# Moving the preparation of two transposed activations in a one-core transformer block: the memory's x^T earlier and later, the residual's x^T columns later

## The chip, the cores and the metric

The kernel runs on one core of a Trainium2 chip. The metric is the device time in microseconds of one execution; the median of three runs is given. The engines are named as in the profile: PE (matrix products), PEld (its weight loads), DVE (vector), ACT (scalar), POOL (general purpose) and SP (which issues most DMAs).

## The reference

One layer of a bidirectional encoder, all in float32, on 256 tokens of width 2048, with 256 memory tokens:

```python
x = x + concat([mla_attention(h), diff_attention(h)]) @ w_out    # h = rms_norm(x)
hx = rms_norm(x, g_xattn);  hm = rms_norm(mem, g_mem)
xq = hx @ w_xq              # (256, 512): queries, 4 heads of 128
xk = hm @ w_xk              # (256, 512): keys of the memory
xv = hm @ w_xv
x = x + softmax(xq xk^T / sqrt(128)) xv @ w_xo
x = x + (silu(hf @ w_gate) * (hf @ w_up)) @ w_down                # hf = rms_norm(x)
return rms_norm(x, g_final)
```

## The kernel before

**Products.** A float32 product is made of three faster ones: every operand is split into a high part, rounded by an ACT cast, and a low part, the rest, by a DVE subtraction, and PE adds high x high, high x low and low x high (lines 99 to 101). The function `split_into` makes the two parts: without a scale at lines 107 (ACT) and 108 (DVE), with a scale at 110 and 111. So each megabyte of weights, once landed in a buffer `wraw` (three of them), passes ACT and DVE as two casts into `wh` and two subtractions into `wl` (four buffers each) before PE can use it. A `wraw` buffer is free for the next DMA when its last subtraction is done.

**Order.** The program is written with tile pools, and the tile framework orders it when it is built: for each engine a planner simulates the time line, follows the order in the program as priority, and takes a later instruction where an earlier one isn't ready in its simulation. The order found is then fixed for each engine. Only the DMAs that SP issues for weights, the memory's x^T and the like are kept in the order of the program (`tc.keep_in_program_order`). Activations live in one pool, `act`, of 24 buffers of 4 KB a partition; a tile waits there until another one is released.

**The stretch that is changed.** The mix of the two attentions is multiplied by `w_out` in two halves of 1024 columns (`wide_add`, h = 0 and 1, called with `mix`). A half runs over eight pairs of 128-row blocks of the weights, in the order `OUT_ORDERS[h]`; for each one `before(n)` is called, then its megabyte is asked for. A pair of kind P is multiplied as it is; one of kind W uses sums of blocks of both operands (the tiles `tsum` and `forms`), which saves products on PE and costs additions on DVE. The half's result is added into the residual `x_res` (`join`, line 365, and `leave`, lines 354 to 362).

Then come the cross attention's keys, `project(mT, w_xk)`, in four pieces of 512 rows, each of them 24 matmuls of 512 columns; the mean squares of the memory's rows (`mss`, from tiles `mn` that POOL's DMAs bring at line 805) and the scaled and transposed keys; then the queries, `project(x1T, w_xq)`, also in four pieces; later the values, `project(mT, w_xv)`.

**What is prepared.** `mT` is the memory's x^T, already transposed in HBM, as four pieces of 512 rows. `mT.load(i)` issues the DMA of piece i on SP (line 408) into an `act` tile `xraw` and splits its four blocks with the gain: four ACT instructions `mT_h` (line 110) and four DVE instructions `mT_l` (line 111). Before, pieces 0, 1 and 2 are loaded ahead of the sixth, seventh and eighth pair of the first half, and piece 3 ahead of the first piece of the keys.

`x1T` is the residual's x^T, made on the chip. `x1_column(oc)` makes 512 rows of it out of 512 columns of `x_res`: for each of two token tiles four transposes on PE into `pt` (line 501), the product with the gain on DVE into `gT` (line 505), the split into `x1T_h` and `x1T_l`, and a square with a sum on ACT (line 203). Column oc is what piece oc of the queries reads. Before, columns 0, 1 and 2 are made ahead of the second, third and fourth piece of the keys and column 3 behind the keys; the reciprocal root of the residual's mean square (`rstdx`, in the profile `x1Tr`: a sum and an addition on DVE, a power on POOL) follows at once and is used when the queries are scaled.

Of the kernel before, what the change touches and what calls it, by code (L numbers as in the profile page):

```python
# [80 lines left out]
def encoder_block(ctx: ExitStack, tc: tile.TileContext, a, out):  # L81
# [15 lines left out]
    def mm(o, l, r, start, stop):  # L97

        nc.tensor.matmul(o, l.h, r.h, start=start, stop=False)  # L99
        nc.tensor.matmul(o, l.h, r.l, start=False, stop=False)  # L100
        nc.tensor.matmul(o, l.l, r.h, start=False, stop=stop)  # L101
# [13 lines left out]
    def act_tile(shape=(P, 4, S), name="act"):  # L115
        return Split(
            act.tile(list(shape), F32R, name=name + "_h", tag="act"),
            act.tile(list(shape), F32R, name=name + "_l", tag="act"),
        )

    def weights(src, fine=False, pool=None, before_k=None, cut=None, raw=None):

        nk, ncols = src.shape[1:]
        begun = raw is not None
        if not begun:
            raw = wp.tile([P, 2048], F32, name="wraw", tag="wraw", bufs=3)
        raw = raw[:, :nk * ncols].rearrange("p (k c) -> p k c", k=nk)  # L130
        step = 1 if fine else nk
        for k in range(0, nk, step):
            if before_k is not None:
                before_k(k)
            if begun and k == 0:
                continue
            tc.keep_in_program_order(nc.sync.dma_start(out=raw[:, k:k + step, :], in_=src[:, k:k + step, :]))
        ks = []
        step = max(1, 1024 // ncols // 2 * 2)
        for k in range(0, nk, step):  # L140
            n = min(step, nk - k)
            if pool:
                w = pool((P, n, ncols), "w")
            else:
                w = [wp.tile([P, 1024], F32R, name=x, tag=x, bufs=4)[:, :n * ncols].rearrange("p (k c) -> p k c", k=n)
                     for x in ("wh", "wl")]
                w = Split(*w)
            if fine:
                for j in range(n):
                    for c in ([slice(0, ncols)] if cut is None or k + j else [slice(0, cut), slice(cut, ncols)]):  # L150
                        split_into(w[:, j, c], raw[:, k + j, c])
            else:
                split_into(w, raw[:, k:k + n, :])
            ks += [w[:, j, :] for j in range(n)]
        return ks

    def project(actT, pieces, before=None, fine=0):

        accs = [acc_tile() for _ in range(NT)]
        ncols = pieces[0].shape[2]  # L160
        nk = sum(src.shape[1] for src in pieces)
        kt = 0
        for i, src in enumerate(pieces):
            if before is not None:
                before(i)
            for w in weights(src, i < fine):
                x = actT(kt)
                for tt in range(NT):
                    mm(accs[tt][:, :ncols], x[tt] if isinstance(x, tuple) else x[:, tt * P:(tt + 1) * P], w,
                       start=kt == 0, stop=kt == nk - 1)  # L170
                kt += 1
        return accs
# [4 lines left out]
    def nat(name):  # L177
        pool, bufs = nat_pool
        return pool.tile([P, 512], F32, name=name, tag="nat", bufs=bufs)
# [4 lines left out]
    def acc_tile(name="acc"):  # L184
        pool, tag = banks[0]
        return pool.tile([P, 512], F32, name=name, tag=tag)
# [5 lines left out]
    def rstd_of(ms, eps, name):  # L192

        cols = ms.shape[-1]
        r = small.tile([P, cols], F32, name=name, tag=name, bufs=2)
        nc.vector.tensor_scalar(out=r, in0=ms, scalar1=eps, scalar2=None, op0=ALU.add)
        nc.gpsimd.tensor_tensor(out=r, in0=r, in1=mhalf[:, :cols], op=ALU.pow)
        return r
# [147 lines left out]
    def wide_add(pairs, src, order, kinds, oc0, done=None, closed=(0, 1), before=None):  # L346


        def x(tt, oc):
            return x_res[tt][:, (oc0 + oc) * 512:(oc0 + oc + 1) * 512]  # L350

        def leave(Q):
            v, u = nat("v"), nat("u")
            nc.scalar.copy(out=u, in_=Q[1])
            nc.vector.tensor_tensor(out=v, in0=Q[6], in1=u, op=ALU.subtract)
            nc.vector.tensor_tensor(out=x(0, 0), in0=x(0, 0), in1=Q[1], op=ALU.add)
            nc.vector.tensor_tensor(out=u, in0=Q[5], in1=v, op=ALU.add)
            nc.vector.tensor_tensor(out=v, in0=v, in1=Q[7], op=ALU.subtract)
            nc.vector.tensor_tensor(out=x(1, 1), in0=x(1, 1), in1=Q[5], op=ALU.add)
            nc.vector.tensor_tensor(out=x(0, 1), in0=x(0, 1), in1=u, op=ALU.add)  # L360
            nc.vector.tensor_tensor(out=x(1, 0), in0=x(1, 0), in1=v, op=ALU.subtract)
            nc.vector.tensor_tensor(out=x(1, 1), in0=x(1, 1), in1=v, op=ALU.add)

        def join(tt, oc, acc):
            nc.vector.tensor_tensor(out=x(tt, oc), in0=x(tt, oc), in1=acc, op=ALU.add)
            if done is not None:
                done(tt, oc0 + oc)

        return wide_project(pairs, src, order, kinds, leave, join, closed, before)
# [236 lines left out]
    acc = project(lambda kt: cqT[:, kt, :], [a["w_uq_r"]])  # L606
# [163 lines left out]
    def column_T(t, oc, tt, gain, ssq, raw=None):  # L770

        xs = x_res[tt][:, oc * 512:(oc + 1) * 512]
        transposed(t, xs, tt, 4, gain[:, 4 * oc:4 * oc + 4], raw)
        meansq(xs, ssq[:, tt, oc:oc + 1], 512, D)

    def rstd_of_sums(ssq, name):
        s1 = small.tile([P, NT], F32, name=name + "s1", tag=name + "s1", bufs=1)
        nc.vector.reduce_sum(out=s1, in_=ssq, axis=AX.X)
        return rstd_of(s1, EPS, name + "r")

    mix = [Pair(t[:, k:k + 2, :]) for t in mixT for k in (0, 2)] + diff
    mT = Transposed(a["memT"], g_m, "mT")
    x1p = []
    x1ss = small.tile([P, NT, 4], F32, name="x1ss", tag="x1ss", bufs=1)
    for h in range(2):
        wide_add(mix, a["w_out"][h], OUT_ORDERS[h], OUT_KINDS[h], 2 * h,
                 before=lambda n: h == 0 and n >= 5 and mT.load(n - 5))

    def x1_column(oc):
        x1p.append(act_tile(name="x1T"))  # L790
        for tt in range(NT):
            column_T(x1p[oc], oc, tt, g_x, x1ss)
# [2 lines left out]
        return x1p[kt // 4][:, kt % 4, :]  # L795


    acc = project(mT, [a["w_xk"][i] for i in range(4)], before=lambda i: x1_column(i - 1) if i else mT.load(3))
    x1_column(3)
    rstdx = rstd_of_sums(x1ss, "x1T")  # L800
    mss = small.tile([P, NT, 4], F32, name="mss", tag="mss", bufs=1)
    for tt in range(NT):
        for c in range(2):
# [8 lines left out]
    for tt in range(NT):  # L812
        n = nat("xk")
# [1 line left out]
        transposed(xkT, n, tt, 4)  # L815


    acc = project(x1T, [a["w_xq"][i] for i in range(4)])
    xqT = act_tile(name="xqT")
    for tt in range(NT):  # L820
        n = nat("xq")
# [113 lines left out]
    for gi, (chunks, order) in enumerate(groups):  # L935
# [49 lines left out]
        for tt in range(NT):  # L985
            for h in range(2):
                acc = acc_tile("acc2")[:, :256]
# [98 lines left out]
```

## Time and profile before

| what | value |
|---|---|
| median of three runs | 1145.25 us (1145.14 to 1145.39) |
| the profiled execution | 1146.86 us, its span 1145.1 us |
| granted PE clock | 0.998 |
| instructions | 14370, 5390 of them matmuls |
| memory's x^T: first and last conversion on ACT | 268.5 and 319.4 us |
| residual's x^T: first and last split on DVE | 343.8 and 360.7 us |
| first matmul of the keys, of the queries | 332.25, 357.89 us |

The span is the time between the first and the last instruction; times within it are counted from its start. A row of the timeline gives the start, the duration, the engine, the line, the operation and the tiles, out<-in; a bracket at its end is the idle time of the engine before it, and what ended it. Rows that follow each other with the same tiles are merged, with their number.

### The profile page before, as it was taken

The page shows a single profiled execution, that of the slowest core. Times are in us where ns is not written, and L with a number is a line of the kernel's source. Part 1 is how long each engine was busy: PE and PEld are TensorE (multiplying, and loading weights), DVE is VectorE, ACT ScalarE, POOL GpSimd, SP SyncE. Part 2 cuts the span into 40 slices and gives each one's busy share as a digit, 9 for nine tenths or more (in the row PEclk, how much of TensorE's full clock was granted, in tenths as well). Part 3 has the DMA queues.
Part 4 walks back from the last instruction along what each step waited for, and adds up shares of the span by engine and source line. Part 5 has one row for each costly group of instructions (what it writes and reads, how often), then busy time and mean ns, then how long its engine had stood idle before and what let it go on. Part 6 is the DMA issues. An engine that isn't in the chain of part 4 may idle for free.

```text
span 1145.1 us, 14370 instructions
## 1 busy us (share of the span) xinstructions
PE 1134.2 (99%) x5390; PEld 947.5 (83%) x5390; DVE 980.3 (86%) x1339; ACT 648.3 (57%) x928; POOL 58.0 (5%) x75
## 2 busy tenths in 40 slices
PE   9999999999999999999999999999999999999997
PEld 7888888887878888888888888888888888888886
DVE  6688766878987767989899998998999898998975
ACT  6755455556556555656455565564554564654642
POOL 4920000000001000000000000000000000000000
PEclk9999999999999999999999999999999999999999
DMA  9655434545557444455555556555555555565553
GB/s 357 217 195 189 144 110 147 185 150 200 202 220 258 150 167 169 177 194 207 197 212 197 181 210 220 184 190 214 184 195 210 207 197 195 193 241 182 204 180 129
DMA packets 34197, 222.13 MB, mean 194 GB/s; under 512 B 4176, under 2 KB 4944, under 8 KB 9808
## 3 DMA queue, kind: packets, MB, share of 16 engines
q1 hardware_dynamic: 32688, 216.73, 53.0%
q0 software_dynamic: 864, 3.15, 0.8%
q10 hardware_dynamic: 576, 1.34, 0.3%
q8 instruction: 42, 0.69, 0.2%
q14 instruction: 27, 0.22, 0.1%
HBM read 219.11 MB, written 2.10 MB: 193 GB/s over the span
## 4 chain that ended last, share of the span: by engine, by line
PE 93%; DVE 4%; DMA 1%; issue 1%; ACT 0%; DVEq 0%; POOLq 0%; POOL 0%; ACTq 0%
PE acc L100 25%; PE acc L101 25%; PE acc L99 25%; PE q L100 3%; PE q L101 3%; PE q L99 3%; DVE wl L108 2%; PE pt L501 2%; DMA wraw<-in_w_dn 1%; PE ppt L649 1%; PE psc L100 1%; PE psc L101 1%; PE psc L99 1%; DVE tsum L301 0%; PE acckv L99 0%
## 5 line engine op out<-in xcount | busy, mean ns | idle before, releaser
L107 ACT CAST wh<-wraw 128x1024 fp32r<-128x1024 f32 (+2 forms) x400 | 389.3, 992 | 334.9 <-PE acc L101 288.7
L108 DVE TENSOR_TENSOR wl<-wraw,wh 128x1024 fp32r<-128x1024 f32 (+2 forms) x400 | 455.0, 1151 | 96.4 <-ACT wh L107 94.8
L107 ACT CAST wh<-tsum 128x1024 fp32r<-128x1024 f32 (+1 forms) x96 | 96.5, 1006 | 56.1 <-PE acc L101 26.0
L100 PE MATMUL acc<-wl,x2n_h 128*128 128x512 f32 x320 | 124.6, 390 | 0.0
L101 PE MATMUL acc<-wh,x2n_l 128*128 128x512 f32 x320 | 123.9, 389 | 0.0
L108 DVE TENSOR_TENSOR wl<-tsum,wh 128x1024 fp32r<-128x1024 f32 (+1 forms) x96 | 111.5, 1164 | 14.2 <-ACT wh L107 13.9
L99 PE MATMUL acc<-wh,x2n_h 128*128 128x512 f32 x320 | 109.7, 391 | 0.0
L100 PE MATMUL acc<-wl,x0T_h 128*128 128x512 f32 x224 | 88.8, 397 | 0.0
L101 PE MATMUL acc<-wh,x0T_l 128*128 128x512 f32 x224 | 88.5, 396 | 0.0
L99 PE MATMUL acc<-wh,x0T_h 128*128 128x512 f32 x224 | 87.5, 398 | 0.8 <-ACT x0T_h L110 0.8
L100 PE MATMUL acc<-wl,hT_h 128*128 128x512 f32 x188 | 73.4, 393 | 0.1
L100 PE MATMUL q<-wl,forms_h 128*128 128x512 f32 x187 | 72.8, 389 | 0.0
L101 PE MATMUL q<-wh,forms_l 128*128 128x512 f32 x187 | 72.6, 389 | 0.0
L101 PE MATMUL acc<-wh,hT_l 128*128 128x512 f32 x188 | 72.4, 390 | 0.0
L100 PEld LDWEIGHTS acc<-wl,x2n_h 128*128 128x128 f32 x320 | 60.1, 188 | 12.3
L101 PEld LDWEIGHTS acc<-wh,x2n_l 128*128 128x128 f32 x320 | 60.1, 188 | 12.4
L99 PEld LDWEIGHTS acc<-wh,x2n_h 128*128 128x128 f32 x320 | 59.9, 188 | 12.3
L99 PE MATMUL q<-wh,forms_h 128*128 128x512 f32 x187 | 65.6, 389 | 0.0
L100 PE MATMUL acc<-wl,forms_h 128*128 128x512 f32 x167 | 64.8, 389 | 0.0
L101 PE MATMUL acc<-wh,forms_l 128*128 128x512 f32 x167 | 64.8, 389 | 0.0
L99 PE MATMUL acc<-wh,hT_h 128*128 128x512 f32 x188 | 64.5, 391 | 0.0
L99 PE MATMUL acc<-wh,forms_h 128*128 128x512 f32 x167 | 62.9, 389 | 0.0
(405 smaller groups left out, 2245.3 us busy)
## 6 DMA issues: line engine op xcount, KB each, us to landing
wraw<-in_w_gate SPq DMA_DIRECT2D x44, 1024.0 KB, 4.8
wraw<-in_w_up SPq DMA_DIRECT2D x44, 1024.0 KB, 4.8
wraw<-in_w_dn SPq DMA_DIRECT2D x41, 1024.0 KB, 4.8
wraw<-in_w_in SPq DMA_DIRECT2D x24, 1024.0 KB, 4.8
wraw<-in_w_out SPq DMA_DIRECT2D x16, 1024.0 KB, 4.8
wraw<-in_w_in_lat SPq DMA_DIRECT2D x7, 832.0 KB, 7.3
wraw<-in_w_xk SPq DMA_DIRECT2D x4, 1024.0 KB, 5.1
wraw<-in_w_xq SPq DMA_DIRECT2D x4, 1024.0 KB, 4.9
```

Source lines behind the costliest of these rows:

```text
L99: nc.tensor.matmul(o, l.h, r.h, start=start, stop=False)
L100: nc.tensor.matmul(o, l.h, r.l, start=False, stop=False)
L101: nc.tensor.matmul(o, l.l, r.h, start=False, stop=stop)
L107: last_cast[0] = nc.scalar.copy(out=dst.h, in_=src).ins
L108: last_split[0] = nc.vector.tensor_tensor(out=dst.l, in0=src, in1=dst.h.bitcast(F32), op=ALU.subtract).ins
L501: nc.tensor.transpose(out=pt[:, j * P:(j + 1) * P], in_=src[:, j * P:(j + 1) * P], identity=ident)
L649: nc.tensor.transpose(out=pt[:, kt * S + tt * P:kt * S + (tt + 1) * P], in_=p[:, tt, kt * P:(kt + 1) * P], identity=ident)
```

## The change

Pieces 0 and 1 of the memory's x^T are loaded ahead of the fourth and the seventh pair of the first half (n = 3 and 6), pieces 2 and 3 ahead of the first and the second piece of the keys. Columns 0 and 1 of the residual's x^T are made ahead of the third and the fourth piece of the keys, columns 2 and 3 ahead of the second and third piece of the queries. The reciprocal root `rstdx` is asked for behind the queries.

```diff
     for h in range(2):
         wide_add(mix, a["w_out"][h], OUT_ORDERS[h], OUT_KINDS[h], 2 * h,
-                 before=lambda n: h == 0 and n >= 5 and mT.load(n - 5))
+                 before=lambda n: h == 0 and n in (3, 6) and mT.load(n // 3 - 1))
...
-    acc = project(mT, [a["w_xk"][i] for i in range(4)], before=lambda i: x1_column(i - 1) if i else mT.load(3))
-    x1_column(3)
-    rstdx = rstd_of_sums(x1ss, "x1T")
+    acc = project(mT, [a["w_xk"][i] for i in range(4)],
+                  before=lambda i: mT.load(i + 2) if i < 2 else x1_column(i - 2))
...
-    acc = project(x1T, [a["w_xq"][i] for i in range(4)])
+    acc = project(x1T, [a["w_xq"][i] for i in range(4)], before=lambda i: i in (1, 2) and x1_column(i + 1))
+    rstdx = rstd_of_sums(x1ss, "x1T")
```

## The prediction

> **What bounds the kernel now.** I read the page first (busy shares, then the chain that ended last), then the table of windows, to find the stretches in which the tensor engine is not full, then that engine's timeline and the chain of waits inside these stretches.
>
> ```profile
> span 1145.1 us, 14370 instructions
> ...
> PE 1134.2 (99%) x5390; PEld 947.5 (83%) x5390; DVE 980.3 (86%) x1339; ACT 648.3 (57%) x928; POOL 58.0 (5%) x75
> ...
> PE 93%; DVE 4%; DMA 1%; issue 1%; ACT 0%; DVEq 0%; POOLq 0%; POOL 0%; ACTq 0%
> ...
> 268.00:285.00 17.00, 16.25 (x70) 12.68 (x69) 16.72 (x28) 15.47 (x26) 0.00 (x0) 1.00 0.33 117
> 285.00:308.00 23.00, 23.00 (x103) 19.00 (x102) 22.26 (x31) 10.37 (x19) 0.00 (x0) 1.00 0.64 224
> 308.00:324.00 16.00, 15.47 (x67) 12.14 (x66) 14.43 (x22) 11.50 (x18) 0.00 (x0) 1.00 0.45 179
> 324.00:360.00 36.00, 36.00 (x175) 29.65 (x174) 33.72 (x46) 21.77 (x32) 3.03 (x5) 1.00 0.65 228
> ```
>
> The columns of a window are its length, then busy time of PE, PEld, DVE, ACT and POOL, the granted clock, and DMA. PE is busy nearly all the time, the chain is PE for 93%, and its clock is whole (1.00). So only what PE stands still for can be won. The change works on the stretch from the wide product with w_out over the memory's keys to the queries; of its windows shown here PE lacks busy time in two only, 268 to 285 and 308 to 324, at the end of either half of the wide product. DVE is nearly full in the first (16.72 of 17.00).
>
> A busy PE need not start matmuls at its rate, so the size of the holes comes from the starts. Timeline of PE, start and duration:
>
> ```profile
> 281.14 0.96 PE L99 MATMUL acc<-wh,diffT_h 128*128 128x512 f32 x3
> ...
> 284.50 0.50 PE L100 MATMUL acc<-wl,diffT_h 128*128 128x512 f32 x1 [0.25 <-DVE wl L108]
> 284.84 0.40 PE L101 MATMUL acc<-wh,diffT_l 128*128 128x512 f32 x1
> ...
> 320.24 0.39 PE L99 MATMUL q<-wh,forms_h 128*128 128x512 f32 x1
> ...
> 320.92 0.39 PE L99 MATMUL q<-pT_h,forms_h 128*128 128x512 f32 x1
> ...
> 323.51 0.50 PE L100 MATMUL acc<-wl,diffT_h 128*128 128x512 f32 x1 [0.39 <-DVE wl L108]
> 323.84 0.40 PE L101 MATMUL acc<-wh,diffT_l 128*128 128x512 f32 x1
> ...
> 332.25 0.61 PE L99 MATMUL acc<-wh,mT_h 128*128 128x512 f32 x2
> ...
> 333.16 0.40 PE L101 MATMUL acc<-wh,mT_l 128*128 128x512 f32 x1
> ```
>
> From 320.24 to 320.92 three matmuls start: 0.227 us each. Stall 1: ten start from 281.14 until 284.84, 3.70 us for 2.27, so 1.43 us are lost. Stall 2: eight from 320.92 until 323.84, 2.92 for 1.82, 1.10 lost. Stall 3, at the first keys: three from 332.25 until 333.16, 0.91 for 0.68, 0.23 lost. Together 2.76 us, 0.24% of the time: more than that the change can't win. 0.2% (2.3 us) is about what a measurement of this kernel can tell from no change.
>
> [...] By PE busy the two windows lack 0.75 + 0.53 = 1.28 us. By weight loads (19.00 of 23.00 in the full window, 12.68 of 17.00 and 12.14 of 16.00 in these) they lack 1.65 and 1.30, 2.95 us. [...]
>
> The chain of waits names what PE waited for:
>
> ```profile
> 269.05 0.97 ACT mT_h L110 x3
> 273.59 1.59 DVE mT_l L111 x4
> ...
> 279.32 0.86 DVE mT_l L111 x3
> ...
> 283.31 1.15 DVE wl L108
> ...
> 312.05 4.89 DMA wraw<-in_w_out
> ...
> 319.53 0.79 DVE mT_l L111 x2
> ...
> 322.32 1.15 DVE wl L108
> ```
>
> Three loads of the memory's x^T (mT, four ACT and four DVE instructions each) stand in front of the split weights (wl) that end stall 1, the fourth load in front of those that end stall 2.
>
> **The change part by part.** One load costs a third of this row, the window of stall 1 for the instructions on the tile xraw alone (length, then DVE and ACT):
>
> ```profile
> 268.00:285.00 17.00, 5.09 (x12) 5.11 (x12) 1.00 0.33 117
> ```
>
> So 1.70 us of DVE and 1.70 of ACT for a load (5.09/3 and 5.11/3).
>
> The queue, and the idle places into which loads move (SP, then DVE, then ACT; the bracket is the idle time before the row):
>
> ```profile
> 246.03 0.42 SPq L408 DMA_DIRECT2D xraw<-in_memT  x1
> 312.43 0.55 SPq L408 DMA_DIRECT2D xraw<-in_memT  x1
> 314.39 0.33 SPq L137 DMA_DIRECT2D wraw<-in_w_xk  x1
> 250.48 1.29 DVE L301 TENSOR_TENSOR tsum<-wraw 128x512 f32<-128x512 f32 x2 [3.66 <-DMA wraw<-in_w_out]
> 267.99 1.38 DVE L108 TENSOR_TENSOR wl<-tsum,wh 128x512 fp32r<-128x512 f32 x2 [1.57 <-ACT wh L107]
> 329.25 0.69 DVE L108 TENSOR_TENSOR wl<-tsum,wh 128x512 fp32r<-128x512 f32 x1 [1.57 <-ACT wh L107]
> 330.35 0.69 DVE L355 TENSOR_TENSOR v<-q,u 128x512 f32<-128x512 f32 x1 [0.41 <-ACT u L354]
> 268.55 1.70 ACT L110 ACTIVATE mT_h<-xraw,gains 128x256 fp32r<-128x256 f32 x4
> 318.23 1.71 ACT L110 ACTIVATE mT_h<-xraw,gains 128x256 fp32r<-128x256 f32 x4 [0.80 <-DMA xraw<-in_memT]
> ```
>
> Load 0, from the sixth pair to the fourth. Its DMA leaves SP ahead of the fourth pair's weights instead of at 246.03; the weights are pushed back by its 0.42 us of issue, or until a buffer of the pool is free, at the latest near 246. Its 1.70 us on DVE then fit before 250.48 (3.66 us idle) or, failing that, are caught up by 267.99 (1.57 idle). Taken: 0.
>
> Load 1 stays at the seventh pair: 0.
>
> Load 2, from the eighth pair to the front of the keys. It leaves stall 1's chain. With load 0 gone too, DVE and ACT have 2 x 1.70 = 3.40 us less to do ahead of the wl at 283.31; one load alone (1.70) would already cover 1.43. Gain of the two: between 0, if the planner's order keeps other work there, and 1.43; taken 1.43, since DVE and ACT work 16.72 and 15.47 of 17.00 us in that window and what leaves is larger than the hole. Late next is the wide product's second half, where DVE works 22.26 of 23.00 us; it enters it ahead by up to 3.40, PE by 1.43, so it doesn't become the bound.
>
> Stall 2: load 2 now has the place in the program and on SP that load 3 had (312.43, right behind the last pair's weights of 312.05), so the same four instructions stand in the same chain. Taken 0 of the 1.10; bounds, a gain of 1.10 if they find another place, a loss as priced under the second rival.
>
> Load 3, from the front of the keys to behind their first piece: its DMA follows the issue of 314.39, its work needs 1.70 us of DVE. Idle there are 1.57 and 0.41 us (329.25 and 330.35), together 1.98. Bounds: 0, if it falls into these, and 1.70, if it comes ahead of the wl that ends stall 3. Taken 0, near the idle time, as its matmuls come last of the four pieces.
>
> The x^T columns of the residual (x1_column): columns 0 and 1 come a piece later among the keys, 2 and 3 go into the queries. Each issues two groups of four transposes, two gains (gT), two casts, two splits and two squares; the number of all of them stays.
>
> ```profile
> 357.11 1.03 PE L501 MATMUL pt<-ident,xres 128*128 128x128 f32 x8
> 357.74 1.29 DVE L505 TENSOR_TENSOR gT<-pt,gains 128x512 f32<-128x512 f32 x2 [0.25 <-PE pt L501]
> 360.08 1.29 DVE L108 TENSOR_TENSOR x1T_l<-gT,x1T_h 128x512 fp32r<-128x512 f32 x2
> 367.46 1.23 DVE L108 TENSOR_TENSOR wl<-wraw,wh 128x1024 fp32r<-128x1024 f32 x1 [1.45 <-ACT wh L107]
> 352.27 0.69 POOL L197 TENSOR_TENSOR x1Tr<-x1Tr,mhalf 128x2 f32<-128x2 f32 x1 [95.70 <-DVE x1Tr L196]
> 352.90 2.40 POOL L805 DMA_DIRECT2D mn<-in_mem  x4
> 379.78 0.60 PE L501 MATMUL pt<-ident,xk 128*128 128x128 f32 x4
> ```
>
> A column takes 360.08 + 1.29 - 357.11 = 4.26 us from transposes to the last split. It is written one piece of the queries ahead of its use, 24 matmuls or 5.45 us, so it has 1.19 us to spare, more if its transposes slip into the keys. Its 2.58 us of DVE fit into idle stretches like that before 367.46 (1.45 us, one for each split). PE does the same transposes. Cost 0, cover: the queries' own matmuls.
>
> The reciprocal root x1Tr goes behind the queries, so the four loads of the memory's rows on POOL (352.90) stand behind it no more and may start earlier. Their squares and the scaled keys end before 379.78, where PE takes them up; earlier loads can only come into the way of other transfers. x1Tr is there some 26 us before 379.78 now and can be late by much of that. Cost 0.
>
> Sum: -1.43 + 0 + 0 + 0. The profiled execution took 1146.86 us (span 1145.1), 1.6 above the median of 1145.25; the difference applies to the median: 1145.25 - 1.43 = **1143.8 us**.
>
> **The rivals.** First, all three stalls go: with DVE 1.70 us lighter up to 324 and the keys' columns later, load 2 falls into idle time of ACT and stall 3 has no column beside it. For it: ACT is busy only 11.50 of 16.00 us there. Against: the load's place in program and queue is the old one. 1145.25 - 2.76 = 1142.5 us.
>
> Second, slower: the two loads side by side at the keys. Load 3's DMA stands behind a piece of weights; the last load's conversion already waited 0.80 us for its DMA (318.23). The 1 MB ahead of load 2 took 4.89 us, and load 2's wait ended 318.23 - 316.94 = 1.3 us behind it; so load 3 lands at about 314.39 + 4.89 + 1.3 = 320.6 (an estimate from these rows). If its conversions are queued right behind load 2's (ACT free at 319.94), ACT stands until 320.6 and then works 1.70: all casts behind are 2.4 us late, and DVE has 1.70 more. The worst is 2.4 + 1.7 = 4.1 us on stalls 2 and 3: 1145.25 - 1.43 + 4.1 = 1147.9 us. It decides once more than 1.43 of the 4.1 reach PE. For it: the order of each engine is planned before the run, and DVE works 33.72 of 36.00 us from 324 on. Against: the gaps for one more load are there. [...]
>
> Third, the change doesn't do what it says: the planner fills the room left in stall 1 with something else, or holds load 0 until a pool buffer comes free and puts it where it was. For it: load 0's DMA was issued at 246.03 and its conversions ran only from 268.55 on, 22.5 us later, where a piece of weights took 4.89 us to land. Even then load 2 has left. 1145.2 us.
>
> Fourth, column 2 or 3 is late for the queries: beyond 1.2 us of spare each further microsecond stalls PE. With two more wl ahead of each (2.46 us, the row of 367.46) it is 1145.25 - 1.43 + 2 x (2.46 - 1.19) = 1146.4 us.
>
> **How the numbers follow.** The forecast 0.47, with a range of its own from 1143.2 to 1144.6; all three stalls gone 0.18; two loads at the keys 0.16; nothing won 0.13; late columns 0.06. Faster by over 0.2% means below 1142.96: the second case, most of it, 0.15. Slower means above 1147.54: the upper part of the slower case, and of an order that breaks elsewhere, 0.12. The rest is within 0.2%: 0.73. The range reaches from 1142.3, all stalls gone, to 1147.3, which leaves 1 in 10 above.
>
> **What would show it.** Right: in the timeline of PE no bracket between 275 and 290, the mT_l of one load alone between 268 and 285, one load before 262, one at about 318 with a stall of about 1 us behind it; the last load's conversions between 322 and 345 with no bracket on PE; gT rows of columns 2 and 3 between 355 and 372 and none of them followed by idle PE. Wrong: a bracket on PE behind a load at the keys, an ACT mT_h waiting longer than 0.8 us for xraw, a bracket on x1T, or DVE full without idle time in 250 to 268 and a new wait on forms.

## The result, and the profile after

The changed kernel takes 1157.56 us (median of four runs, 1156.65 to 1158.18), the kernel before 1145.2 beside it: ratio 1.0106, 95% interval 1.0094 to 1.0119. It is 12.4 us slower. The forecast was 1143.8, and the range ended at 1147.3. The profiled execution took 1157.55 us.

The page of the changed kernel, first lines and chain:

```profile
span 1155.4 us, 14368 instructions
...
PE 1137.4 (98%) x5390; PEld 949.2 (82%) x5390; DVE 980.7 (85%) x1339; ACT 648.6 (56%) x928; POOL 57.2 (5%) x75
...
PE 95%; DMA 1%; ACT 1%; DVE 1%; issue 1%; SPq 0%; DVEq 0%; POOLq 0%; POOL 0%; ACTq 0%
```

The page hardly tells it: the work of DVE and ACT is what it was (980.3 and 648.3 us before), and PE is even busier, 3.2 us more for the same matmuls. The windows show why (length, busy PE, PEld, DVE, ACT and POOL, each with its number of instructions, granted clock, DMA share, GB/s):

```profile
260.00:264.00 4.00, 1.26 (x6) 0.70 (x4) 3.47 (x10) 3.42 (x9) 0.00 (x0) 1.00 0.00 0
264.00:268.00 4.00, 3.19 (x8) 2.52 (x9) 3.92 (x6) 3.17 (x4) 0.00 (x0) 0.52 0.00 0
268.00:271.00 3.00, 3.00 (x9) 2.32 (x8) 3.00 (x5) 0.88 (x2) 0.00 (x0) 0.51 0.90 311
271.00:285.00 14.00, 14.00 (x63) 11.60 (x62) 12.69 (x21) 8.98 (x15) 0.00 (x0) 1.00 0.55 186
285.00:308.00 23.00, 23.00 (x103) 19.03 (x103) 22.22 (x29) 14.03 (x21) 0.00 (x0) 1.00 0.62 215
308.00:324.00 16.00, 16.00 (x72) 13.27 (x71) 12.46 (x17) 7.01 (x10) 2.41 (x4) 1.00 0.61 228
324.00:329.00 5.00, 2.65 (x11) 1.66 (x10) 3.70 (x7) 4.25 (x8) 0.00 (x0) 1.00 1.01 419
329.00:332.40 3.40, 3.40 (x9) 2.62 (x9) 3.40 (x5) 3.21 (x7) 0.00 (x0) 0.50 0.63 196
```

Stall 1 is gone (271 to 308 is full). There are two holes instead, and behind each the granted clock is half. Hole 1, near 261, is new. Hole 2, near 325, is stall 2 grown: in both kernels PE stands around the diffT products at the end of the second half, which the kernel before took up at 321.46. Half a clock counts as busy PE: the nine matmuls of 329 to 332.4 would have taken 2.04 us at the 0.227 us from start to start of the full clock. The starts on PE, with the brackets, and then that row of the kernel before:

```profile
260.87 0.40 PE L101 MATMUL acc<-wh,mixT_l 128*128 128x512 f32 x1
264.81 2.07 PE L99 MATMUL acc<-wh,mixT_h 128*128 128x512 f32 x4 [3.54 <-ACT wh L107]
266.68 0.63 PE L100 MATMUL acc<-wl,mixT_h 128*128 128x512 f32 x1
...
270.94 0.41 PE L101 MATMUL acc<-wh,mixT_l 128*128 128x512 f32 x1
...
324.71 0.39 PE L101 MATMUL q<-wh,forms_l 128*128 128x512 f32 x1
327.45 1.20 PE L99 MATMUL acc<-wh,diffT_h 128*128 128x512 f32 x4 [2.35 <-ACT wh L107]
...
339.57 0.61 PE L99 MATMUL acc<-wh,mT_h 128*128 128x512 f32 x2
340.60 0.50 PE L100 MATMUL acc<-wl,mT_h 128*128 128x512 f32 x1 [0.41 <-DVE wl L108]
...
375.81 1.04 PE L501 MATMUL pt<-ident,xres 128*128 128x128 f32 x8
378.10 0.66 PE L501 MATMUL pt<-ident,xres 128*128 128x128 f32 x4 [1.25 <-DVE gT L505]
...
381.22 0.50 PE L101 MATMUL acc<-wh,x1T_l 128*128 128x512 f32 x1 [0.83 <-DVE x1T_l L108]
```

```profile
321.46 1.20 PE L99 MATMUL acc<-wh,diffT_h 128*128 128x512 f32 x4
```

By starts of 0.227 us: hole 1, 15 matmuls from 260.87 until 270.94, 10.07 us for 3.41, **6.66 lost**, 3.71 of them standing and the rest at half clock. Hole 2, 15 matmuls from 324.71 until PE is back at its rate at 332.51, 7.80 for 3.41, **4.39 lost**, 2.51 of them standing. The late columns lose **2.4 to 2.6** between 376 and 381, stall 3 **0.69** (it was 0.23). Together 14.2 us where the kernel before lost 2.76: 11.4 more, of the 12.4 measured. (The spans differ by 10.3 only, since the profiled execution of before was 1.6 above its median; 1.2 of that lies ahead of this stretch, where the same matmuls start 1.2 us later in it.)

What stood in the way in hole 1: ACT's timeline of the changed kernel, one row of SP, and then, in a fence of its own, ACT of the kernel before.

```profile
234.21 18.50 SPq L211 DMA_DIRECT2D wraw<-in_w_out  x3
...
259.24 0.27 ACT L241 COPY a<-pdt 128x128 f32<-128x128 f32 x1 [5.78 <-PE pdt L741]
...
262.11 1.71 ACT L110 ACTIVATE mT_h<-xraw,gains 128x256 fp32r<-128x256 f32 x4
263.71 3.45 ACT L107 CAST wh<-wraw 128x1024 fp32r<-128x1024 f32 x4
```

```profile
255.46 2.01 ACT L107 CAST wh<-wraw 128x1024 fp32r<-128x1024 f32 x2 [0.29 <-PE acc L101]
...
263.87 0.37 ACT L107 CAST forms_h<-pdt 128x256 fp32r<-128x256 f32 x1 [1.36 <-DVE sums L245]
```

The fourth pair's weights were asked for at 234.21 and took 4.8 us to land. In the kernel before their casts run at 255.46, ahead of the forms. Now ACT stands idle for 5.78 us until PE has made the input of the copy (pdt), and makes the copy, the forms and all of load 0's conversions first: the fixed order has the casts behind them, those of the fifth pair too. So it is not a late transfer but an order. Why the planner ordered it so, no run shows.

Hole 2 comes from a late transfer. SP, POOL and ACT of the changed kernel:

```profile
315.43 1.92 SPq L408 DMA_DIRECT2D xraw<-in_memT  x1
318.38 0.45 SPq L408 DMA_DIRECT2D xraw<-in_memT  x1
...
315.30 1.34 POOL L804 DMA_DIRECT2D mn<-in_mem  x2 [60.81 <-ACT wh L107]
320.86 1.07 POOL L804 DMA_DIRECT2D mn<-in_mem  x2 [4.22 <-PE acc L101]
...
324.75 1.71 ACT L110 ACTIVATE mT_h<-xraw,gains 128x256 fp32r<-128x256 f32 x4 [3.30 <-DMA xraw<-in_memT]
```

The memory's rows (mn) are fetched from 315.30 on, not from 352.90, together with the last weights of w_out and two xraw; load 2's xraw is there 9.3 us after its issue (324.75 - 315.43), and ACT waits 3.30 us for it, with the casts that PE needs queued behind.

### The profile page after: what moved, and what is told of

Same layout as the page of the kernel before. It is cut to its first block, busy times and chain, and to the rows that moved or that the text cites. A ratio compares the mean times of both kernels' runs of the same rounds, so it can differ in the third digit from the quotient of the medians.

```text
span 1155.4 us, 14368 instructions
## 1 busy us (share of the span) xinstructions
PE 1137.4 (98%) x5390; PEld 949.2 (82%) x5390; DVE 980.7 (85%) x1339; ACT 648.6 (56%) x928; POOL 57.2 (5%) x75
## 3 DMA queue, kind: packets, MB, share of 16 engines
q10 hardware_dynamic: 576, 1.34, 0.3%
## 4 chain that ended last, share of the span: by engine, by line
PE 95%; DMA 1%; ACT 1%; DVE 1%; issue 1%; SPq 0%; DVEq 0%; POOLq 0%; POOL 0%; ACTq 0%
PE acc L99 25%; PE acc L100 25%; PE acc L101 25%; PE q L100 4%; PE q L101 4%; PE q L99 4%; PE pt L501 2%; DMA xraw<-in_memT 1%; PE ppt L649 1%; PE psc L100 1%; PE psc L101 1%; PE psc L99 1%; ACT wh L107 1%; DMA wraw<-in_w_in_lat 0%; DVE wl L108 0%
## 5 line engine op out<-in xcount | busy, mean ns | idle before, releaser
L101 PEld LDWEIGHTS acc<-wh,x2n_l 128*128 128x128 f32 x320 | 60.1, 188 | 12.4
```

## The experiments

The theory has three causes, each with a place. Load 0's DMA in SP's kept order puts the casts behind the forms (hole 1); mn, fetched early, takes the DMA engines from xraw (hole 2); columns 2 and 3 are late at the queries. Its rivals are load 0's conversions as such, two loads side by side at the keys, and the new order of DVE and ACT. Times are medians, beside the kernel before on the same chip (1145.3 to 1145.6). Loads 0 and 1 "put back" means the sixth and seventh pair; load 1 was at the seventh in the changed kernel too, so only load 0 moves.

| kernel | median, us | ratio to before, 95% |
|---|---|---|
| load 0 alone | 1152.69 | 1.0059 (1.0043 to 1.0076) |
| loads 2, 3 at the keys alone | 1144.25 | 0.9990 (0.9981 to 0.9999) |
| columns and root alone | 1154.88 | 1.0081 (1.0066 to 1.0096) |
| changed, loads 0, 1 put back | 1151.80 | 1.0055 (1.0040 to 1.0070) |
| load 0's DMA on POOL | 1145.95 | 1.0004 (0.9995 to 1.0014) |
| columns late, mn on SP | 1152.22 | 1.0059 (1.0044 to 1.0074) |
| columns late, keys' scaling behind | 1154.01 | 1.0074 (1.0059 to 1.0089) |
| load 2 in the second half | 1146.33 | 1.0006 (0.9997 to 1.0016) |
| changed, columns 2, 3 put back | 1150.65 | 1.0046 (1.0032 to 1.0060) |
| the same, loads 0, 1 put back too | 1144.46 | 0.9991 (0.9982 to 1.0000) |
| loads 2, 3 at the keys alone, again | 1144.38 | 0.9991 (0.9982 to 1.0000) |
| changed loads, load 0 on POOL, columns as before | 1144.92 | 0.9995 (0.9986 to 1.0003) |

### Each part by itself

Load 0 alone:

```diff
-  before=lambda n: h == 0 and n >= 5 and mT.load(n - 5))
+  before=lambda n: h == 0 and n in (3, 6, 7) and mT.load({3: 0, 6: 1, 7: 2}[n]))
```

> The kernel before with load 0 alone moved to the fourth pair (loads 1 and 2 stay at the seventh and eighth, keys and columns as before). Theory (load 0's move alone makes the hole near 261 us: the weights' casts of the next pairs go behind the forms, PE stands over 3 us, and its clock is then halved for 6.83 us): a hole of 3 to 4 us before a first product with wh near 260 to 265, granted clock 0.5 behind it, 7 us in all, less at most the 1.43 us of stall 1: 1150.8 to 1152.3 us. Rival (the hole comes with what the other parts moved, load 0 is harmless by itself as predicted): no bracket there and 1143.8 to 1145.3 us.

Measured 1152.69, 0.4 above the expected range. The hole is there (PE stands 3.71 us too long before 265.4, then half a clock to about 268.6), so the rival falls. The hole cost less than the 7 us of the expectation, some 5.3 by the starts, because the clock was half for only about 3.4 us. What made up the sum is a wait of 1.61 us on a split weight at the keys (339.13), which the expectation didn't have.

Loads 2 and 3 at the keys alone:

```diff
+  before=lambda n: h == 0 and n in (5, 6) and mT.load(n - 5))
...
+  before=lambda i: (i < 2 and mT.load(i + 2), i and x1_column(i - 1)))
```

> The kernel before with loads 2 and 3 at the first two pieces of the keys, loads 0 and 1 at the sixth and seventh pair, the columns and the reciprocal root as before, so the four loads of the memory's rows (mn) leave POOL after 350 us. Theory (the hole near 325 us is the transfers': xraw lands in 9.3 us since mn is under way beside it): xraw lands within 6 us, no hole over 1.5 us between 320 and 340, clock whole; stall 1 goes: 1143.8 to 1145.2 us. Rival (two loads side by side at the keys make the hole by themselves, as the prediction's second rival has it): ACT waits over 2 us for xraw near 320 to 325, a hole of 2 us or more and half a clock behind it, 1146.5 to 1148.5 us.

Measured 1144.25, as the theory had it: the two loads side by side do no harm. mn is fetched from 350.86 on, xraw lands in 6.5 us (median of the two, a little over the 6 expected), and ACT waits 0.65 us for load 2.

The columns and the root alone:

```diff
+  before=lambda i: mT.load(3) if i == 0 else i > 1 and x1_column(i - 2))
...
+  before=lambda i: i in (1, 2) and x1_column(i + 1))
+  rstdx = rstd_of_sums(x1ss, "x1T")
```

> The kernel before with the columns a piece later and two of them at the queries, the reciprocal root behind the queries, all four loads of the memory's x^T as before. Theory (columns 2 and 3 come at their use, 2.4 to 2.8 us lost between 376 and 381 us; and mn, now issued near 315 us, delays the one load at the keys): 1148.0 us from the columns alone, up to 4.4 us more if load 3 is delayed as in the changed kernel: 1147.5 to 1152.5 us, with brackets on gT between 374 and 382. Rival (the columns are late only because the keys were late in the changed kernel; alone they have their 1.19 us to spare): 1144.5 to 1145.7 us.

Measured 1154.88, more than either sum: a hole near 320 with only one load at the keys. On SP the order is that of the kernel before throughout, and on ACT it differs only behind the copy u, which ran at 329.73 there. So up to the hole only mn has moved. The brackets on gT are there as expected (1.25 us at 376.17). The keys are late here too, so the time alone doesn't refute the rival; the order on PE does, in the part on the prediction below. ACT and PE of this kernel, then the transfers issued from 310 to 330 (KB each, us to landing), first of this kernel and then of the one before:

```profile
322.10 1.71 ACT L110 ACTIVATE mT_h<-xraw,gains 128x256 fp32r<-128x256 f32 x4 [4.88 <-DMA xraw<-in_memT]
322.83 0.50 PE L100 MATMUL q<-wl,forms_h 128*128 128x512 f32 x1 [2.42 <-DVE wl L108]
```

```profile
mn<-in_mem POOLq DMA_DIRECT2D x3, 512.0 KB, 5.9
wraw<-in_w_out SPq DMA_DIRECT2D x1, 1024.0 KB, 7.7
xraw<-in_memT SPq DMA_DIRECT2D x1, 512.0 KB, 9.2
```

```profile
wraw<-in_w_out SPq DMA_DIRECT2D x1, 1024.0 KB, 4.9
xraw<-in_memT SPq DMA_DIRECT2D x1, 512.0 KB, 5.8
```

The last weights of w_out land 2.8 us later, xraw 3.4. PE waits for the split of the one, and ACT stands behind the other.

The changed kernel with loads 0 and 1 at the sixth and seventh pair again (`n in (5, 6) and mT.load(n - 5)`):

> The changed kernel with loads 0 and 1 back at the sixth and seventh pair; all else as changed. Theory (the first hole belongs to load 0's move alone): it is gone, stall 1 stays gone, the hole near 325 and the late columns stay: 1157.6 - 7.1 = 1150.5 us, 1149.5 to 1151.5. Rival (what makes the hole is load 2's leaving or the planner's new order as a whole): the hole near 261 stays, 1156.5 to 1158.5 us.

Measured 1151.80: hole 1 is gone, the window from 240 to 268 full. That is 1.3 above the expected 1150.5 and 0.3 above its range. Hole 2 is larger (starts 1.18 and 2.07 us late before 323.6, then half a clock, some 5.0 us in all for 4.39), and, against the expectation, 0.7 us of stall 1 is back; stall 3 is back at its 0.23.

### What carries it

Load 0 alone again, but its DMA issued by POOL, so that SP's order of the weights is the old one:

```diff
-  tc.keep_in_program_order(nc.sync.dma_start(out=raw[:, :n, :], in_=self.src[i, :, k:k + n, :]))
+  (nc.gpsimd.dma_start(out=raw[:, :n, :], in_=self.src[i, :, k:k + n, :]) if self.name == "mT" and i == 0 else
+   tc.keep_in_program_order(nc.sync.dma_start(out=raw[:, :n, :], in_=self.src[i, :, k:k + n, :])))
```

> Load 0 alone at the fourth pair, as in the run of that part alone, but its DMA issued by POOL instead of SP; the weights' DMAs on SP are then in the order that they had before. Theory (it is the place of load 0's DMA in SP's kept order, in front of the fourth pair's weights, that puts the casts of the fourth and fifth pair behind the forms): the casts wh run before the forms again, no hole near 261 us, clock whole, 1144.0 to 1145.6 us. Rival (the priority of load 0's conversions in the program takes ACT and DVE away from the weights): the hole stays, 1151.5 to 1153 us.

Measured 1145.95, 0.35 above the expected range. POOL and ACT:

```profile
255.13 0.79 POOL L408 DMA_DIRECT2D xraw<-in_memT  x1
...
254.12 2.00 ACT L107 CAST wh<-wraw 128x1024 fp32r<-128x1024 f32 x2 [0.29 <-PE acc L101]
...
262.54 0.37 ACT L107 CAST forms_h<-pdt 128x256 fp32r<-128x256 f32 x1 [1.36 <-DVE sums L245]
```

The casts are ahead of the forms again and the hole is gone. The limit of this run is in the first row: POOL issued the load only at 255.13, so its conversions could not come early either, and the rival isn't excluded by it. A second sign: with only the DMA at the fourth pair and the conversions left at the sixth, the order that is built is that of load 0 alone on every engine, but for buffers' numbers. So the DMA's place gives that order without the conversions' place. That kernel wasn't run.

The columns late, mn issued by SP behind the keys' weights:

```diff
-  nc.gpsimd.dma_start(out=mn, in_=a["mem"][tt * P:(tt + 1) * P, c * 1024:(c + 1) * 1024])
+  tc.keep_in_program_order(nc.sync.dma_start(out=mn, in_=a["mem"][tt * P:(tt + 1) * P, c * 1024:(c + 1) * 1024]))
```

> The columns and the reciprocal root late, the four loads of the memory's x^T as before, and the four loads of the memory's rows (mn) issued by SP behind the keys' weights instead of by POOL. Theory (the hole near 320 us in the run of the late columns is contention of mn's transfers with xraw and the last weights of w_out, and nothing else): xraw lands in about 5.8 us again, the hole of 2.4 us and the half clock behind it go; what stays is the late columns' 2.4 to 2.8 us and stalls 1 to 3: 1147.5 to 1148.5 us. Rival (the new order of DVE and ACT makes the hole): it stays and 1153 to 1156 us.

Measured 1152.22, above the theory's time, but not by its hole: near 320 only stall 2 is left. First its ACT near 317 and PE near 359; then PE of the next kernel, with the scaling of the keys behind the queries:

```profile
316.87 1.71 ACT L110 ACTIVATE mT_h<-xraw,gains 128x256 fp32r<-128x256 f32 x4 [0.74 <-DMA xraw<-in_memT]
...
358.86 0.48 PE L501 MATMUL pt<-ident,xk 128*128 128x128 f32 x1 [3.80 <-DVE xk L813]
```

```profile
385.48 0.87 PE L501 MATMUL pt<-ident,xk 128*128 128x128 f32 x3 [6.15 <-DVE xk L816]
```

With mn out of the way ACT waits 0.74 us for xraw (0.80 before), and up to there the orders of SP, ACT, DVE and PE are those of the run of the columns alone, which has the hole: there it is mn's. The cost is elsewhere: the keys' transposes stand first in PE's order and wait for the squares of mn, which ACT does one after another from 350.84 to 356.85. The clock is half behind this hole too, from about 357.6 to 364.4.

> The columns and the reciprocal root late, the loads of the memory's x^T as before, and the memory's squares with the scaling and transposing of the keys moved behind the queries in the program, so that columns 2 and 3 come ahead of them. Theory (the program's place of that block, ahead of columns 2 and 3, lets mn take buffers early and puts the columns' transposes behind the keys' on PE): mn is issued after 345 us, no hole near 320, no bracket on gT at the queries: 1145.0 to 1146.0 us. Rival (columns one piece ahead of their use are late by themselves): 2.4 to 2.8 us of brackets on gT between 368 and 382 us, 1147.5 to 1148.5 us.

Its edit moves the block from `mss` to the keys' transposes behind the queries' project. Measured 1154.01, above the theory's range and the rival's. As the theory has it, mn is issued at 353.76, hole 2 is gone and no gT holds up PE. But the keys are now late: ACT ends the last squares at 383.35, and PE stands 6.15 us before 385.48.

### Put back, one place at a time

The changed kernel with columns 2 and 3 in front of the memory's squares:

```diff
   acc = project(mT, [a["w_xk"][i] for i in range(4)],
                 before=lambda i: mT.load(i + 2) if i < 2 else x1_column(i - 2))
+  x1_column(2)
+  x1_column(3)
...
-  acc = project(x1T, [a["w_xq"][i] for i in range(4)], before=lambda i: i in (1, 2) and x1_column(i + 1))
+  acc = project(x1T, [a["w_xq"][i] for i in range(4)])
```

> The changed kernel with one thing put back: columns 2 and 3 stand behind the keys in the program, in front of the memory's squares, instead of among the queries. Columns 0 and 1 stay a piece later, the root stays behind the queries, all four loads stay as changed. Theory (the place of columns 2 and 3 behind the memory's squares in the program makes both the second hole, through mn's early transfers, and the brackets on gT; the root's place and the two loads at the keys are harmless): mn leaves POOL after 345 us, no hole over 1.5 us after 300, only the hole near 261 stays: 1150.8 to 1153 us. Rival (the root's place on POOL, or columns 0 and 1, or load 0's delay of everything behind it makes them): 1154.5 to 1158 us.

And with loads 0 and 1 at the sixth and seventh pair as well:

> The same, with loads 0 and 1 back at the sixth and seventh pair as well. Theory (two places make the whole loss: load 0's on SP, and columns 2 and 3 behind the memory's squares): no hole over 1.5 us anywhere from 240 to 400, 1143.8 to 1145.0 us. Rival (columns 0 and 1 a piece later, or the root, cost something of their own): 1146 to 1149 us.

Measured 1150.65 (0.15 under the expected range) and 1144.46. In the first mn leaves POOL at 358.07, load 2's xraw lands in 5.9 us instead of 9.3, and hole 2 is gone. This is the cleanest test of it: the orders of SP, ACT, DVE and PE are those of the changed kernel until well behind the hole (ACT's is the first to differ, at 343 us of the changed kernel), so of what can reach the hole only mn has moved. POOL and the windows of the second:

```profile
350.66 2.20 POOL L197 TENSOR_TENSOR x1Tr<-x1Tr,mhalf 128x2 f32<-128x2 f32 x1 [94.61 <-DVE x1Tr L196]
352.81 2.40 POOL L806 DMA_DIRECT2D mn<-in_mem  x4
```

```profile
240.00:262.00 22.00, 22.00 (x116) 18.70 (x115) 17.73 (x29) 13.07 (x23) 1.69 (x2) 1.00 0.46 165
262.00:268.00 6.00, 6.00 (x30) 4.95 (x29) 3.86 (x10) 2.78 (x6) 0.00 (x0) 1.00 0.71 272
268.00:285.00 17.00, 16.84 (x74) 13.37 (x73) 16.73 (x26) 13.36 (x22) 0.00 (x0) 1.00 0.39 131
...
308.00:324.00 16.00, 15.58 (x69) 12.57 (x68) 14.72 (x21) 11.60 (x21) 0.00 (x0) 1.00 0.51 198
```

The whole loss splits. Each kernel against the kernel before beside it: the changed one loses 12.4 us, with columns 2 and 3 put back 5.2, with load 0 put back too it gains 1.0. So columns 2 and 3 behind the memory's squares cost 12.4 - 5.2 = 7.2 us (hole 2 and the late columns), load 0's place 5.2 + 1.0 = 6.2 (hole 1), and the rest of the change gains 1.0. Load 0 put back first, in the run further up, gives 5.9 for its part.

It also says something on why mn came early. In this kernel the root still follows the queries in the program, and yet POOL does x1Tr first and mn from 352.81. So the root's place in the program is not what let mn go early; the place of columns 2 and 3 is. What held mn is open: on POOL it left as x1Tr ended (350.66 + 2.20), so the trace can't tell x1Tr from a wait of its own. mn's tiles come from the pool of the activations, and in the kernel before the columns stood ahead of them in the program. That the pool's buffers are what mn gets from the columns fits, but no run separates it from the rest of the program's order.

### Is there more to win

> The kernel before with loads 2 and 3 at the first two pieces of the keys, as run already, with more rounds beside the next kernel: 1143.7 to 1145.0 us, 0.05 to 0.15% under the kernel before.

> All four loads as changed, but load 0's DMA issued by POOL so that SP's order in front of the fourth pair stays, and the columns and the root as before. Theory (with load 0's DMA off SP the first hole goes, and with the columns as before the second): stalls of 0.5 to 1.5 us in all from 240 to 400, 1143.5 to 1145.0 us. Rival (two loads more to convert beside the columns' work at the keys): 1145.5 to 1147 us.

> Loads 0 and 1 at the sixth and seventh pair of the first half, load 2 at the fourth pair of the second half, load 3 and the columns as before. The theory (each load costs only what its place in the plan costs; one load less shortens stall 1, and nothing else moves): stall 1 gone or under 0.6 us, stall 2 as before at 1.1 us, 1144.0 to 1144.8 us. Rival (DVE is the bound of the second half, 22 of 23 us busy from 285 to 308, so its 1.70 us comes back there): 1145.3 to 1147 us, with a bracket on a split weight before 324.

The first has the edit shown for it, the second the loads of the change with POOL's DMA for load 0 and the columns and root of before; the third:

```diff
-  before=lambda n: h == 0 and n >= 5 and mT.load(n - 5))
+  before=lambda n: (h == 0 and n in (5, 6) and mT.load(n - 5)) or (h == 1 and n == 3 and mT.load(2)))
```

Measured 1144.38, 1144.92 and 1146.33: the first two as expected, the third inside its rival's range. It has a hole of 1.34 us (PE, then ACT):

```profile
299.36 0.50 PE L99 MATMUL q<-wh,forms_h 128*128 128x512 f32 x1 [1.34 <-ACT wh L107]
...
291.70 1.30 ACT L110 ACTIVATE mT_h<-xraw,gains 128x256 fp32r<-128x256 f32 x3
...
297.65 0.63 ACT L203 ACTIVATE junk<-xres 128x512 bf16<-128x512 f32 x1
...
298.28 1.03 ACT L107 CAST wh<-wraw 128x1024 fp32r<-128x1024 f32 x1
```

The load's conversions at 291.70 put ACT behind, and three squares of xres stand in front of the cast. The wait is on ACT, not on DVE as its rival said. Loads 2 and 3 at the keys, with the rest as before or as in the kernel with both places put back, are the best seen: 0.1% under the kernel before, at the edge of what the intervals can tell.

## Why the prediction was wrong

**Load 2 off stall 1, taken 1.43: right in kind, half the size.** With two loads at the keys alone 0.70 us of stall 1 stays, so 0.73 is won there, and stall 2 shrinks from 1.10 to 0.7 to 0.8, where nothing was forecast. The run gains 1.1 us. That the forecast would have been nearly right for this part is partly luck. In the changed kernel all of stall 1 is gone, but with load 0 moved as well.

**Two loads side by side, the slower rival: wrong mechanism.** By themselves they cost nothing measurable. What was feared of load 3's xraw befell load 2's, through a transfer that this rival did not count; so stall 2, taken as unchanged at 1.10, grew to the 4.39 of hole 2. What it did have right is the queue: in hole 2 ACT waits 3.30 us for xraw, and the casts behind it in ACT's order wait as well, so that PE waits 2.35 us for one of them.

**Load 0, taken 0: the first step that failed.** Its price was worked out as 0.42 us of issue and 1.70 us of work with idle time for both. But the order of each engine is fixed from the plan, and the DMA's place ahead of the fourth pair's weights on SP put the casts of two pairs behind other work (263.71 instead of 255.46): hole 1, 6.66 us by the starts and 6.2 by putting it back. The step asked where load 0's instructions would fit, not what the plan would do with those behind its DMA. The third rival came near ("holds load 0 until a pool buffer comes free"), but let only load 0 wait.

**mn, "earlier loads can only come into the way of other transfers", taken 0: the second.** The sentence named the mechanism and gave it no price. It was there to be worked out: mn brings four times 512 KB into a stretch where xraw already made ACT wait 0.80 us, and half of that is as much again as the weights ahead of load 2, which took 4.89 us. What it cost, 4.39 for 1.10, hole 2 shows. The reason given for an earlier mn, the root's new place, was not enough either: with the root behind the queries and columns 2 and 3 in front, mn left POOL at 352.81.

**Columns with 1.19 us to spare, taken 0: the third.** The 4.26 us of the chain fit, but they were counted from "a piece ahead of use". On PE the fixed order has the columns' transposes behind those of the keys and behind the queries' second piece, thus right at their use, whenever the keys come. In the run of the columns alone, where that piece ends at 373.0:

```profile
373.01 1.04 PE L501 MATMUL pt<-ident,xk 128*128 128x128 f32 x8
373.89 1.04 PE L501 MATMUL pt<-ident,xres 128*128 128x128 f32 x8
```

The fourth rival's 2 x 1.27 = 2.5 us is what they lost, 2.4 to 2.6, though by another road: that agreement is luck.

**The range.** Every stall was priced by the time that PE stands. Half a clock came on top: some 3 us in hole 1, nearly 2 in hole 2. The chances don't quite fit each other either: with 0.12 for more than 1147.54, the chance above the range's end at 1147.3 can't be less, so "1 in 10" is too small.

## What to carry to other kernels

Where a planner fixes each engine's order, moving a DMA in a kept queue moves everything behind it in the plan: price the instructions that depend on the transfers behind it, not only the moved ones. Before work is moved later in the program, look for what may take its buffers and its transfers' place, and price the newcomer's bytes at the moment of the tightest load. On a PE that is full, the two holes of the changed kernel, 3.71 and 2.51 us of standing, cost 6.66 and 4.39 us here, with half a clock behind them for about 6.8 and 3.4 us; the casts out of place in hole 1 alone outweighed the three stalls of the kernel before, 2.76 us together.

## What the runs showed of the hardware

The granted clock fell to 0.50 with every hole that lost over 2 us in one piece in these runs, for one of two lengths by the windows. About 3.4 us: hole 2 of the changed kernel (329.0 to 332.4), load 0 alone (265.2 to 268.6), and the changed kernel with loads 0 and 1 put back, whose hole lost 2.07 us in one piece (324.3 to 327.7). About 6.8: hole 1 of the changed kernel (264.1 to 270.9), the columns alone (0.66 on the mean of 324 to 334), the columns late with mn on SP (357.6 to 364.4) or with the keys' scaling behind (0.77 on the mean of 375 to 390), and columns 2 and 3 put back (0.68 on the mean of 262 to 268, 0.91 from 268 to 285). The late columns, whose 2.4 to 2.6 us are spread over several waits, left it whole in the changed kernel (1.00 from 376 to 382).

The same 3.71 us lost near 261 cost 6.8 us of half clock in the changed kernel (the 0.52 and 0.51 of its windows), but about 3.4 in the run of load 0 alone, where the clock was 0.71 from 268 to 269 and whole from there. After 2.35 us of idle PE (hole 2) it was about 3.4. Single waits of 1.61 us (load 0 alone, at the keys) and 1.34 us (load 2 in the second half) left it whole, 1.00 in their windows. Why the same hole cost one length in one run and twice that in another, no run shows.
